# A hybrid attention and GLA block: copies and adds of output-weight blocks queued behind weight loads and probability scalings

## The chip, the cores and the metric

The kernel runs on one core of one Trainium2 chip. The metric is the device time of one execution in microseconds (us). Three executions of the kernel before took 952.4, 955.09 and 950.05 us; their median is 952.4 us. The engines are TensorE (PE, with its weight loads as PEld), VectorE (DVE), ScalarE (ACT), GpSimd (POOL) and SyncE (SP). In this kernel SP issues nearly all transfers, and POOL issues those that add to what lies at the destination.

## What is computed

One layer over 512 tokens of width 2048, all in float32:

```
mod = silu(c) @ w_cond + b_cond            -> shift, scale, gate
h   = rms_norm(x) * (1 + scale) + shift
proj = h @ w_in                            -> aq ak av ag gq gk gv gg lr_f lr_b
A: dilated window attention, 16 heads x 64, three patterns, relative bias; times silu(ag)
B: gated linear attention (GLA), 4 heads, forward and backward; normed, times silu(gg)
y   = concat(A, B) @ w_out                 (512x2048 @ 2048x2048)
out = rms_norm(x + gate * y) * final_gain
```

## The kernel before

**Arithmetic.** Every large product is made of three float32r products: each operand is split into a high part (a rounded copy, made on ACT) and a low part (the rest, made on DVE), and the helper `three` (lines 214 to 217) issues high by high, high by low and low by high.

**Stages.** A first stage works through `w_cond` and the first two weight sets (sa, sb). Then come ten units, each a projection of 512 columns: qk2, qk4, qk6, gk, gv0, gv1, ag0, ag1, gg0, gg1. The function `unit` (line 1000 on) runs a unit in eight groups of two 128-row blocks of weights. At each group it splits the weights of this group and the next (`split_hi` on ACT, `split_lo` on DVE) and asks for the weight loads of the groups two and three ahead (`fetch`, on SP). A unit has 64 ticks, one for each set of three products; at given ticks it issues other work, its side list:

- in qk2, qk4, qk6 and gk the attention of four heads each: scores (L723, L724), softmax (DVE L727, ACT L730, DVE L731), the scaling of the probabilities `p` by the inverse sum on POOL (L735), a transpose on PE (L747) and the products with the values (L761);
- in gv1, ag0, ag1 and gg0 one GLA head each (`gla_head`), with decay products `dc` on POOL (L923);
- from qk6 on, sums for the value bias and the gate (`some_sums`): loads of `rawv` and `rawg` on SP (L831, L797), consumed on DVE (L836, L314);
- in all ten units the block sums described below.

At the start of each unit with attention the heads' keys are laid out: `ks` and `kl` are written in one half of the partitions and carried to the other half by two small transfers on SP (L696, L698). The scores read them.

**The output product and the block sums.** The last stage multiplies by `w_out` with Strassen-like sums: per pair of column blocks seven products, of whose weights four (T1 to T4) are sums and differences of blocks of `w_out`. The blocks are summed in device memory: `sum_start` (L392, on SP) copies 512 KB from a source into a new buffer T, `sum_add` (L397, on POOL) adds a second block to it by a transfer that accumulates. T1 and T3 start from `w_out` itself, T2 from T1, T4 from T2; with two pairs and four row groups there are 32 copies and 32 adds. They stand in one list `sum_ops`, in steps, so that an add or a dependent copy comes some places after what it needs. `SUM_OPS_IN` deals the list out to the units, and `unit` issues the share evenly over its 64 ticks.

**What sets the order.** PE's instructions run in the order of the program. Those of the other engines and queues are put in order by a planner at build time, which may move an instruction ahead of others on its queue when by its own times it is ready and the queue is free; side work is issued with raised priority. The executed order is then fixed: each queue issues in order, and an instruction that waits holds up all behind it.

The list has 64 entries: gv0 and gg1 get 5, ag1 and gg0 get 6, the other six units 7 each.

Of the kernel before, what the change touches and what calls it, by code (L numbers as in the profile page):

```python
# [14 lines left out]
ALU = mybir.AluOpType  # L15
# [105 lines left out]
OUT_SUMS = {"T1": ("11", "12"), "T3": ("12", "22"), "T2": ("T1", "22"), "T4": ("T2", "21")}  # L121
# [57 lines left out]
def block_kernel(ctx: ExitStack, tc: tile.TileContext, a: dict):  # L179
    nc = tc.nc  # L180
# [12 lines left out]
    def T2(name, dt=F32, parts=P):  # L193
        return t2.tile([parts, 512], dt, tag="t2", name=name)

    def B8(name, shape, dt=F32):
        return b8.tile([P] + shape, dt, tag="b8", name=name)
# [4 lines left out]
    def PA(name):  # L202
        return pp.tile([P, 512], F32, tag="pa", bufs=3, name=name)
# [41 lines left out]
    def RAW(name, shape):  # L245
        return wp.tile([P] + shape, F32, tag="raw", bufs=4, name=name)
# [100 lines left out]
    groups = [(u, g) for u in order for g in range(KT // 2)]  # L347
    groups += [("O", s) for s in range(2 * 4 * len(OUT_ORDER))]
    gi = {ug: i for i, ug in enumerate(groups)}
    raws, wts, low = {}, {}, set()  # L350

    def fetch(i):
        if i < len(groups) and i not in raws:
            u, g = groups[i]
            if u == "O":
                raws[i] = out_fetch(g)
            else:
                raws[i] = RAW(f"raw_{u}{g}", [2, 512])
                nc.sync.dma_start(raws[i], a["w_" + u][g])

    def out_block(pair, which, g):

        l, r = OUT_PAIRS[pair]
        j, z = {"11": (l, g), "21": (l, 4 + g), "12": (r, g), "22": (r, 4 + g)}[which]
        return a[f"w_o{j}"][z]

    def out_fetch(s):

        pair, q = divmod(s, 4 * len(OUT_ORDER))
        what, g = OUT_WEIGHTS[OUT_ORDER[q // 4]], q % 4  # L370
        if s % 2 and s >= OUT_DEEP:
            t = op.tile([P, 2, 512], F32, tag="raw", bufs=3, name=f"raw_O{s}")
        else:
            t = RAW(f"raw_O{s}", [2, 512])
        if what in OUT_SUMS:
            d = dsum[pair, what, g]
            nc.sync.dma_start(t.rearrange("p k c -> p (k c)"),
                              bass.AP(d.tensor, d.offset, [[1024, P], [1, 1024]]))
        else:
            nc.sync.dma_start(t, out_block(pair, what, g))  # L380
        return t

    dsum = {}

    def flat(t):
        return bass.AP(t.tensor, t.offset, [[2048, 64], [1, 2048]])

    def sum_start(pair, name, g):
        def go():
            src = OUT_SUMS[name][0]  # L390
            dsum[pair, name, g] = t = dp.tile([64, 2048], F32, tag=f"{name}{pair}{g}", name=f"{name}{pair}{g}")
            nc.sync.dma_start(t, flat(dsum[pair, src, g] if src in OUT_SUMS else out_block(pair, src, g)))  # L392
        return go

    def sum_add(pair, name, g):
        def go():
            nc.gpsimd.dma_start(dsum[pair, name, g], flat(out_block(pair, OUT_SUMS[name][1], g)), accum_op=ALU.add, max_dma_last_dim=8192)  # L397
        return go

    sum_ops = []  # L400
# [23 lines left out]
    def split_hi(i):  # L424
        if i < len(groups) and i not in wts:
            fetch(i)
            u, g = groups[i]
            raw = raws[i].rearrange("p k c -> p (k c)")
            dst = None
            if (u, g) == ("O", len(groups) - gi["O", 0] - 4):  # L430
                t = b8.tile([P, 2, 1024], F32R, tag="b8", name="wlast")
                dst = t[:, 0, :], t[:, 1, :]
            wts[i] = dst or (wp.tile([P, 1024], F32R, tag="whi", name=f"{u}{g}h"),
                             wp.tile([P, 1024], F32R, tag="wlo", name=f"{u}{g}l"))
            act(wts[i][0], raw, AF.Copy)
# [182 lines left out]
    for z in range(2):  # L618
        for e in range(3):
            name = ("mm", "a", 0, 7) if (z, e) == (1, 2) else ("m0", z, e)  # L620
# [3 lines left out]
    for i in range(n):  # L624
        if i > 7:
            mm_task(i)
        st, k, j = chain[i]
# [15 lines left out]
    for i in range(n, 2 * n):  # L643
        mm_task(i)
        st, k, j = chain[i]
# [3 lines left out]
    for w in range(4):  # L649
        for kt in range(4):  # L650
            j, g = w // 2 * 4 + kt, w % 2
# [51 lines left out]
    def attention(pairs):  # L703

        tiles = [(2 * p + j, i) for p in pairs for j in range(2) for i in range(4)]
        gt, pt, pr_ = {}, {}, {}
        heads = [2 * p + j for p in pairs for j in range(2)]

        def g_load(h):
            g = gp.tile([P, 896], F32, tag="g", name=f"g{h}")  # L710
            nc.sync.dma_start(g, bass.AP(grow.tensor, grow.offset + h * 1024, [[1, P], [1, 896]]))
            gt[h] = g

        def score(h, i):
            def go():
                if h % 8 == 0 and i == 0:
                    cat[h // 8] = B8(f"cat{h // 8}", [4, 512])
                if i == 1 and h != heads[-1]:
                    g_load(h + 1)
                qs, ks, kl, _ = stacks[h]  # L720
                q = slice(P * i, P * i + P)
                ps = PA(f"s{h}{i}")
                mm(ps, qs[:, q], ks, start=True, stop=False)  # L723
                mm(ps, qs[:, q], kl, start=False, stop=True)  # L724
                t = T2(f"p{h}{i}")
                st = sm.tile([P, 3], F32, tag="st", name=f"st{h}{i}", bufs=6)
                nc.vector.tensor_tensor_reduce(  # L727
                    out=t, in0=ps, in1=gt[h][:, P * i:P * i + 512], op0=ALU.add, op1=ALU.min,
                    scale=1.0, scalar=3e38, accum_out=st[:, 0:1])
                act(t, t, AF.Exp, bias=st[:, 0:1], scale=-1.0, accum_out=st[:, 1:2])  # L730
                nc.vector.reciprocal(st[:, 2:3], st[:, 1:2])  # L731
                if (h, i) in ((15, 2), (15, 3)):
                    act(t, t, AF.Copy, scale=st[:, 2:3])
                else:
                    nc.gpsimd.tensor_scalar(t, t, st[:, 2:3], 1.0, op0=ALU.mult, op1=ALU.mult)  # L735
                pr_[h, i] = t
            return go

        def turn(h, i):
            def go():  # L740
                half, ii = divmod(i, 2)
                if ii == 0:
                    pt[h, half] = B8(f"pt{h}{half}", [2, 4, 256], F32R)
                t = pr_.pop((h, i))
                pk = PA(f"t{h}{i}")
                for kt in range(4):
                    nc.tensor.transpose(pk[:, kt * P:kt * P + P], t[:, kt * P:kt * P + P], ident)  # L747
                hi = pt[h, half][:, 0, :, P * ii:P * ii + P]
                lo = pt[h, half][:, 1, :, P * ii:P * ii + P]
                src = pk.rearrange("p (k q) -> p k q", k=4)  # L750
                act(hi, src, AF.Copy)  # L751
                tt(lo, src, hi.bitcast(F32), op=ALU.subtract)  # L752
            return go

        def values(h, half):
            def go():
                t = pt.pop((h, half))
                po = PA(f"o{h}{half}")
                for kt in range(4):
                    for w in range(2):  # L760
                        mm(po[:, :256], vv[h // 4][:, kt, h % 4, :], t[:, w, kt, :],  # L761
                           start=kt == 0 and w == 0, stop=kt == 3 and w == 1)
                oh = sm.tile([64, 256], F32, tag="oh", name=f"oh{h}{half}", bufs=1)
                act(oh, po[64:128, :256], AF.Copy)  # L764
                own = stacks[h][3]
                p = h // 2
                dst = cat[p // 4][own, p % 4, 256 - 256 * half:512 - 256 * half]
                tt(dst[:, ::-1], po[0:64, :256], oh, op=ALU.add)  # L768
            return go

        items = []
        n = len(tiles)
        for x in range(n + 4):
            if x < n:
                items.append(score(*tiles[x]))
            if 2 <= x <= n + 1:
                items.append(turn(*tiles[x - 2]))
            if x == n:
                continue
            for v in (x - 4, x - 3) if x == n + 1 else (x - 3,):  # L780
                if 0 <= v < n and tiles[v][1] % 2 == 1:
                    items.append(values(tiles[v][0], tiles[v][1] // 2))
        g_load(heads[0])
        start, span, move0, move1, move_last = ATT_AT
        at = [start + (q + 0.5) / len(items) * span for q in range(len(items))]
        at[0] -= move0
        at[1] -= move1
        at[-1] += move_last
        return list(zip(at, items))
# [366 lines left out]
    for e in "hl":  # L1156
        t = hp.tile([P, KT, 512], F32R, tag="h", name="c_" + e)
# [263 lines left out]
```

## Time and profile before

| | |
|---|---|
| median of three runs | 952.4 us |
| profiled execution | 955.71 us, span 953.9 us |
| granted PE clock, mean | 0.988 |
| PE busy | 922.7 us, 97% of the span |
| DVE, ACT, POOL busy | 656.1, 473.3, 84.5 us |
| SP's transfers (q1) | 191.61 MB, 57.0% of 16 DMA engines |
| POOL's transfers (q0) | 16.84 MB, 9.1% of 16 DMA engines |

The profiled execution lies 3.3 us above the median. Times in a trace count from the start of the span. A row of the timeline gives start, length, engine, line, operation, output and inputs, and in brackets how long the engine had been idle and what ended that. A row of waits gives the total, the number of times and the longest. A row of stages gives the stretch, its length, the busy time of PE, PEld, DVE, ACT and POOL, the granted clock, the share of the DMA engines and GB/s.

### The profile page before, as it was taken

How to read it: one execution, taken by the hardware profiler on the slowest of the kernel's cores; microseconds unless marked ns; L12 is line 12 of the kernel's file. 1: busy time of each engine (PE TensorE's matmuls, PEld its weight loads, DVE VectorE, ACT ScalarE, POOL GpSimd, SP SyncE). 2: the span in 40 equal slices, each digit the busy share in tenths (PEclk: the TensorE clock that was granted, in tenths of full speed). 3: DMA queues.
4: the chain of work that ended last, by engine and by line, in shares of the span. 5: the costliest groups of instructions: out<-in, count | busy, mean ns of one | idle time of the engine just before them, and what ended most of it. 6: DMA issues, size and time to landing. Idle time of an engine off the chain costs nothing.

```text
span 953.9 us, 12126 instructions
## 1 busy us (share of the span) xinstructions
PE 922.7 (97%) x4375; PEld 763.3 (80%) x4375; DVE 656.1 (69%) x960; ACT 473.3 (50%) x770; POOL 84.5 (9%) x120
## 2 busy tenths in 40 slices
PE   8999999989899979999999999999999999999996
PEld 6888888868677858888887888888888888888884
DVE  7988899746555647676643566578597628798486
ACT  5543533635445535565621545454364428555464
POOL 0000000112413312212100000000001000000001
PEclk9999999989999989999999999999999999999998
DMA  9999496979999998353245425355455446966853
GB/s 353 403 411 366 190 366 232 277 211 287 287 291 278 292 265 269 117 174 127 98 156 177 135 76 169 97 176 179 156 173 168 136 138 224 320 210 223 279 173 138
DMA packets 52803, 209.79 MB, mean 220 GB/s; under 512 B 7204, under 2 KB 7492, under 8 KB 45960
## 3 DMA queue, kind: packets, MB, share of 16 engines
q1 hardware_dynamic: 49680, 191.61, 57.0%
q0 software_dynamic: 2624, 16.84, 9.1%
q8 instruction: 34, 0.56, 0.2%
q10 hardware_dynamic: 440, 0.57, 0.2%
q14 instruction: 25, 0.20, 0.1%
HBM read 200.53 MB, written 37.83 MB: 250 GB/s over the span
## 4 chain that ended last, share of the span: by engine, by line
PE 56%; DVE 3%; DMA 1%; issue 1%; ACT 1%; ACTq 0%; DVEq 0%
PE g L217 4%; PE g L216 4%; PE g L215 4%; PE ps_gv L217 3%; PE ps_gv L216 3%; PE ps_gv L215 3%; PE ps_ag L215 3%; PE ps_ag L217 3%; PE ps_ag L216 3%; PE ps_gg L215 2%; PE ps_gg L216 2%; PE ps_gg L217 2%; PE o L761 2%; PE ps_gk L217 2%; PE ps_gk L215 2%; PE ps_gk L216 2%
## 5 line engine op out<-in xcount | busy, mean ns | idle before, releaser
L730 ACT ACTIVATE p<-p,st 128x512 f32<-128x512 f32 x64 | 46.1, 721 | 72.5 <-DVE st L727 70.6
L314 DVE CUSTOM_DVE_ANT_0 cb<-cb,sb,c_bcond 128x2048 f32<-128x2048 f32 (+1 forms) x32 | 73.5, 2296 | 1.5 <-DMA cb<-in_wm 1.2
L727 DVE CUSTOM_DVE_ANT_0 p<-s,g 128x512 f32<-128x512 f32 x64 | 43.9, 688 | 32.6 <-PE s L724 32.4
L735 POOL TENSOR_SCALAR p<-p,st 128x512 f32<-128x512 f32 x62 | 49.3, 808 | 129.3 <-DVE st L731 99.0
L752 DVE TENSOR_TENSOR pt<-t,pt 128x512 fp32r<-128x512 f32 x64 | 43.8, 689 | 21.5 <-ACT pt L751 21.0
L751 ACT ACTIVATE pt<-t 128x512 fp32r<-128x512 f32 x64 | 37.9, 592 | 14.9 <-PE t L747 13.9
L747 PEld LDWEIGHTS t<-c_ident,p 128*128 128x128 f32 x256 | 31.7, 142 | 16.5 <-POOL p L735 8.6
L747 PE MATMUL t<-c_ident,p 128*128 128x128 f32 x256 | 39.6, 278 | 5.6 <-POOL p L735 5.3
L397 POOL DMA_DIRECT2D T<-in_w_o x32 | 25.6, 800 | 202.5 <-DMA T<-in_w_o 131.5
L761 PEld LDWEIGHTS o<-pt,vv 128*128 128x128 f32 x256 | 34.8, 188 | 2.8
L761 PE MATMUL o<-pt,vv 128*128 128x256 f32 x256 | 35.5, 281 | 0.0
L723 PE MATMUL s<-ks,qs 128*128 128x512 f32 x64 | 26.2, 409 | 7.6 <-DMA ks<-ks 7.5
L923 POOL TENSOR_SCALAR dc<-st,sc 128x256 f32<-128x256 f32 x16 | 9.4, 586 | 249.2 <-DVE st L920 244.2
L724 PE MATMUL s<-kl,qs 128*128 128x512 f32 x64 | 26.2, 410 | 4.4 <-DMA kl<-kl 4.3
L314 DVE CUSTOM_DVE_ANT_0 rawg<-rawg,sb,gate 128x1024 f32<-128x1024 f32 x16 | 20.5, 1282 | 13.5 <-DMA rawg<-in_wg 13.4
L731 DVE RECIPROCAL st<-st 128x1 f32<-128x1 f32 x64 | 10.3, 161 | 24.8 <-ACT p L730 24.8
L314 DVE CUSTOM_DVE_ANT_0 rawg<-rawg,sb,c_bcond 128x1024 f32<-128x1024 f32 x16 | 20.5, 1281 | 6.7 <-DMA rawg<-in_wg 6.7
L1246 POOL TENSOR_SCALAR x<-x,rn 128x512 f32<-128x512 f32 x3 | 3.4, 1137 | 216.6 <-ACT rn L1235 216.6
L723 PEld LDWEIGHTS s<-ks,qs 128*128 128x128 f32 x64 | 12.4, 194 | 12.0 <-issue 7.1
L930 ACT ACTIVATE sq<-st,sc 128x256 f32<-128x256 f32 x24 | 12.2, 508 | 18.6 <-DVE st L925 9.3
L768 DVE TENSOR_TENSOR cat<-o,oh 64x256 f32<-64x256 f32 x32 | 13.3, 416 | 8.3 <-ACT oh L764 7.8
L314 DVE CUSTOM_DVE_ANT_0 rawv<-rawv,shb,vbias 128x1024 f32<-128x1024 f32 x8 | 10.2, 1281 | 12.7 <-DMA rawv<-in_wv 12.6
(1519 smaller groups left out, 2976.1 us busy)
## 6 DMA issues: line engine op xcount, KB each, us to landing
cb<-in_wm SPq DMA_DIRECT2D x31, 1024.0 KB, 8.4
T<-in_w_o POOLq DMA_DIRECT2D x32, 512.0 KB, 9.7
rawg<-in_wg SPq DMA_DIRECT2D x32, 512.0 KB, 3.3
raw_O<-T SPq DMA_DIRECT2D x32, 512.0 KB, 4.9
raw_qk<-in_w_qk SPq DMA_DIRECT2D x24, 512.0 KB, 7.9
raw_O<-in_w_o SPq DMA_DIRECT2D x24, 512.0 KB, 4.2
rawb<-in_w_sb SPq DMA_DIRECT2D x16, 512.0 KB, 5.2
T<-in_w_o SPq DMA_DIRECT2D x16, 512.0 KB, 9.8
```

Of the source, the lines that this page charges most:

```text
L215: mm(ps, lh, rh, start=first, stop=False, skip_group_check=more)
L216: mm(ps, ll, rh, start=False, stop=False, skip_group_check=more)
L217: mm(ps, lh, rl, start=False, stop=last, skip_group_check=more)
L314: nc.vector.tensor_tensor_reduce(out=w, in0=w, in1=with_, op0=ALU.mult, op1=ALU.add, scale=1.0, scalar=init, accum_out=dst)
L723: mm(ps, qs[:, q], ks, start=True, stop=False)
L727: nc.vector.tensor_tensor_reduce(out=t, in0=ps, in1=gt[h][:, P * i:P * i + 512], op0=ALU.add, op1=ALU.min, scale=1.0, scalar=3e38, accum_o ...
L730: act(t, t, AF.Exp, bias=st[:, 0:1], scale=-1.0, accum_out=st[:, 1:2])
L735: nc.gpsimd.tensor_scalar(t, t, st[:, 2:3], 1.0, op0=ALU.mult, op1=ALU.mult)
L747: nc.tensor.transpose(pk[:, kt * P:kt * P + P], t[:, kt * P:kt * P + P], ident)
L751: act(hi, src, AF.Copy)
L752: tt(lo, src, hi.bitcast(F32), op=ALU.subtract)
L761: mm(po[:, :256], vv[h // 4][:, kt, h % 4, :], t[:, w, kt, :], start=kt == 0 and w == 0, stop=kt == 3 and w == 1)
```

## The change

Two entries are kept in `last`: the last weight load that `fetch` issued in the program's order, and the last scaling of probabilities. A copy is tied behind the first on SP, an add behind the second on POOL. The tie (`tc.issue_after`) is one of order on the queue alone; nothing waits on a signal that it did not wait on before. The planner may still place the copy or add anywhere later on the queue.

```
-    raws, wts, low = {}, {}, set()
+    raws, wts, low, last = {}, {}, set(), {}
...
-                nc.sync.dma_start(raws[i], a["w_" + u][g])
+                last["load"] = nc.sync.dma_start(raws[i], a["w_" + u][g]).ins
...
     def sum_start(pair, name, g):
...
-            nc.sync.dma_start(t, flat(dsum[pair, src, g] if src in OUT_SUMS else out_block(pair, src, g)))
+            with tc.issue_after(last["load"]):
+                nc.sync.dma_start(t, flat(dsum[pair, src, g] if src in OUT_SUMS else out_block(pair, src, g)))
...
     def sum_add(pair, name, g):
         def go():
-            nc.gpsimd.dma_start(dsum[pair, name, g], flat(out_block(pair, OUT_SUMS[name][1], g)), accum_op=ALU.add, max_dma_last_dim=8192)
+            with tc.issue_after(last["pool"]) if "pool" in last else nullcontext():
+                nc.gpsimd.dma_start(dsum[pair, name, g], flat(out_block(pair, OUT_SUMS[name][1], g)),
+                                    accum_op=ALU.add, max_dma_last_dim=8192)
...
-                    nc.gpsimd.tensor_scalar(t, t, st[:, 2:3], 1.0, op0=ALU.mult, op1=ALU.mult)
+                    last["pool"] = nc.gpsimd.tensor_scalar(t, t, st[:, 2:3], 1.0, op0=ALU.mult, op1=ALU.mult).ins
```

After gk there is no further scaling, so the adds of the later units are tied to the last one of gk. The loads of the output product's own weights don't count as `last["load"]`.

## The prediction

> **What bounds the kernel now.** I read the page's busy shares first, then the busy time stage by stage, then the waits of TensorE (PE) where the stages differ, and last the queues that feed them.
>
> ```profile
> PE 922.7 (97%) x4375; PEld 763.3 (80%) x4375; DVE 656.1 (69%) x960; ACT 473.3 (50%) x770; POOL 84.5 (9%) x120
> ```
>
> PE is busy for 922.7 of 953.9 us, so only its holes and its clock can be won. The next rows cut the span into units: qk2, qk4, qk6 and gk (each a projection with the attention of four heads inside), gv0 with gv1, ag0 with ag1, gg0 with gg1.
>
> ```profile
> 188.50:267.00 78.50, 70.64 (x346) 57.96 (x346) 44.01 (x91) 39.30 (x75) 22.04 (x30) 0.93 0.93 264
> 267.00:337.40 70.40, 67.08 (x354) 55.67 (x353) 42.26 (x89) 37.68 (x72) 20.77 (x28) 1.00 1.02 290
> 337.40:412.60 75.20, 68.82 (x354) 56.79 (x353) 46.84 (x97) 37.71 (x73) 15.01 (x20) 0.95 0.68 206
> 412.60:479.00 66.40, 66.37 (x354) 55.87 (x353) 45.17 (x97) 37.49 (x72) 9.73 (x14) 1.00 0.42 134
> 479.00:585.00 106.00, 106.00 (x502) 86.85 (x501) 52.76 (x68) 39.04 (x60) 1.92 (x4) 1.00 0.43 138
> 585.00:693.00 108.00, 108.00 (x541) 91.62 (x540) 72.84 (x100) 52.64 (x87) 3.84 (x8) 1.00 0.47 155
> 693.00:798.00 105.00, 104.62 (x493) 87.03 (x491) 69.87 (x88) 50.40 (x71) 3.63 (x4) 1.00 0.45 147
> ```
>
> The columns after the length are busy time of PE, PEld, DVE, ACT and POOL, then granted PE clock, DMA share and GB/s. The first four units hold nearly the same PE work (354 matmuls in the records of three of them), yet take 78.5, 70.4, 75.2 and 66.4 us. Against the last, the first three lose 12.1 + 4.0 + 8.8 = 24.9 us. Of that, PE is idle for 7.86 + 3.32 + 6.38 = 17.56 us (length less busy); the other 7.3 us is a lower clock (0.93 and 0.95). Their DMA share is 0.93, 1.02 and 0.68, against 0.42 in gk. What ends the holes, from the waits of PE between 180 and 365 us, and three of the holes:
>
> ```profile
> PE s L723 <- DMA ks<-ks: 7.5, 3, 4.3
> PE t L747 <- POOL p L735: 5.3, 4, 1.9
> PE s L724 <- DMA kl<-kl: 4.3, 1, 4.3
> ...
> 199.18 0.76 PE L723 MATMUL s<-ks,qs 128*128 128x512 f32 x1 [4.34 <-DMA ks<-ks]
> 257.84 0.66 PE L747 MATMUL t<-c_ident,p 128*128 128x128 f32 x4 [1.91 <-POOL p L735]
> 303.88 0.66 PE L747 MATMUL t<-c_ident,p 128*128 128x128 f32 x4 [1.93 <-POOL p L735]
> ```
>
> So 11.8 us wait for small SBUF-to-SBUF transfers (ks, kl) and 5.3 us for POOL's scaling of probabilities. Both trace to the block sums, which are all issued between 168 and 367 us:
>
> ```profile
> L397 POOL DMA_DIRECT2D T<-in_w_o x32: 762/782/1068, 173.5 to 367.1; - x32
> DMA to landing us min/median/max: 7.6/9.7/14.6
> ...
> L392 SPq DMA_DIRECT2D T<-in_w_o x16: 489/539/691, 168.5 to 299.6; - x16
> L392 SPq DMA_DIRECT2D T<-T x16: 467/516/1475, 212.5 to 355.9; - x16
> ...
> 255.82 0.78 POOL L397 DMA_DIRECT2D T<-in_w_o  x1 [9.52 <-DMA T<-T]
> 275.34 0.77 POOL L397 DMA_DIRECT2D T<-in_w_o  x1 [13.59 <-DMA T<-T]
> ```
>
> An add at the head of POOL's queue waits for its copy to land (9.52, 13.59 us) while scalings stand behind it; the hole at 257.84 follows the first of these. And the ks transfer, to landing, in the gk stage (405 to 425 us) and then around qk6 (325 to 360 us):
>
> ```profile
> DMA to landing us min/median/max: 2.2/2.3/2.4
> DMA to landing us min/median/max: 8.1/12.2/14.4
> ```
>
> 2.3 us where no sum is under way, 12.2 us where the DMA engines are full.
>
> **The change part by part.** No work is added or removed: 32 copies (SP) and 32 adds (POOL) stay, in the same list, dealt out as 7, 7, 7, 7, 5, 7, 7, 6, 6, 5 to the ten units. Each copy now stands on SP behind the weight load traced last, each add on POOL behind the scaling traced last. The load traced last is two or three groups ahead of PE, a group being 66.4 / 8 = 8.3 us, so a copy can run at most some 25 us ahead of its place; the adds of the attention units can't pass a scaling. So 28 of the 64 operations stay in the four attention units, 36 go to gv0 and after.
>
> *DMA load.* Against gk's 0.42 the first three units carry (0.93 × 78.5 + 1.02 × 70.4 + 0.68 × 75.2) − 0.42 × 3 × 66.4 = 196 − 84 = 112 us of engine time for about 57 operations (64 less some 7 issued before 188 us), 2 us each. Seven to a unit of 66.4 us then add 14 / 66.4 = 0.21: the attention units fall to about 0.63, gk rises to the same, and the units from gv0 on, 36 × 2 = 72 us more over 319 us, go from 0.45 to 0.68. No stage stays full.
>
> *ks and kl.* At 0.63 I estimate 4 to 6 us to landing: between 2.3 and 12.2, nearer the first, since a queue that is not full empties between operations. The three holes in qk4 and qk6, 11.8 − 4.34 = 7.5 us, begin late after the issue; the first of each:
>
> ```profile
> 264.11 0.48 SPq L696 DMA_DIRECT2D ks<-ks  x1
> 335.08 0.48 SPq L696 DMA_DIRECT2D ks<-ks  x1
> ...
> 275.47 0.47 PE L723 MATMUL s<-ks,qs 128*128 128x512 f32 x1 [1.24 <-DMA ks<-ks]
> 346.75 0.47 PE L723 MATMUL s<-ks,qs 128*128 128x512 f32 x1 [1.95 <-DMA ks<-ks]
> ```
>
> PE came at 274.2 and 344.8, some 10 us after the issue. With 6 us to landing all 7.5 us go. In qk2 the cover is thinner:
>
> ```profile
> 186.03 0.49 SPq L392 DMA_DIRECT2D T<-in_w_o  x1
> 189.29 0.51 SPq L696 DMA_DIRECT2D ks<-ks  x1
> ...
> 185.43 0.81 POOL L397 DMA_DIRECT2D T<-in_w_o  x1 [11.12 <-DMA T<-in_w_o]
> 187.91 0.77 POOL L397 DMA_DIRECT2D T<-in_w_o  x1 [1.67 <-DMA T<-in_w_o]
> 194.84 0.77 POOL L397 DMA_DIRECT2D T<-in_w_o  x1 [6.16 <-DMA T<-in_w_o]
> ```
>
> PE came at 199.18 − 4.34 = 194.84, 5.55 us after the issue at 189.29. A copy three microseconds ahead of ks stays about where it is; the adds of 185.43, 187.91 and 194.84 go to the second half of the unit. Bounds: 0 (all of the wait goes) and 4.34 us plus its share of the clock (it stays). I take 1.0 us as what is left here.
>
> *Scalings.* An add now follows its copy by 4 to 10 places of the list in the attention units (about 9.5 us a place, 66.4 / 7), 38 us or more, against a longest copy of 18.1 us to landing:
>
> ```profile
> DMA to landing us min/median/max: 4.1/11.3/18.1
> ```
>
> So no add waits in front of a scaling, and the 5.3 us go. What an add itself takes on POOL stays: 12 adds of 0.78 us in the attention units, at most 9.4 us if each held PE up and nothing if the 56.7 idle us of POOL in gk (66.4 − 9.73) hide them; I take nothing, since some 28 adds stand among the scalings today and every hole but one of 0.45 us follows an add that waited.
>
> *Clock.* The lower clock follows the holes; with them gone the 7.3 us come back. At one place the row and the notes can be weighed:
>
> ```profile
> 260.00:280.00 20.00, 18.70 (x86) 15.23 (x84) 11.61 (x20) 9.87 (x17) 3.50 (x6) 0.93 1.03 247
> 300.00:320.00 20.00, 18.07 (x99) 15.04 (x98) 10.65 (x26) 10.18 (x21) 6.71 (x9) 1.00 1.00 299
> ```
>
> The hole of 1.91 us at 257.84 is followed by a clock of 0.93, that of 1.93 us at 303.88 by none lost. The Trainium skill, "TensorE: Matmul & The Clock Gate", Part 1, has the clock halved after an idle window of about 3.4 us and full again after a busy one; the trace agrees that holes come first, but a hole of 1.9 us was enough once. By that page three drops at half rate would be worth an estimated 3 × 1.7 = 5.1 us instead of 7.3 and the time 2.2 us higher; I keep the rows.
>
> *Copies on SP.* A copy occupies SP for 0.54 us and may wait there. A T<-T copy must wait for the add before it in the chain of sums, and loads queue behind it. Between add and copy stand at least 5 places but for the last two (4 and 3), more than 28 us; less the 25 us ahead and the 9.7 us of an add, a few could wait some microseconds. The cover is the same two or three groups that the loads run ahead: I take 0. Without that cover the loads would be late for PE, which is the fourth rival.
>
> *The later units.* Here 36 operations are new. PE has no hole from 479 to 693 us and 0.38 us from 693 to 798, but the chain of work passes through DVE and two waits for gate weights:
>
> ```profile
> 681.55 4.62 DMA rawg<-in_wg
> ...
> 687.51 3.15 DMA rawg<-in_wg
> ...
> 715.26 0.55 PE kt L901 x3
> ```
>
> A load takes 3.15 us alone and 4.62 us behind another. A copy in between will stretch some. DVE waits in order, so its weight splits and the gates of the next GLA head come later. Bounds: 0, and for the five units two loads each stretched by 4.62 − 3.15 = 1.5 us and all of it on PE's path, 15 us. PE's full rows before 693 say that most heads have room, this one none: I take 2.5 us. POOL's decay products (dc) could stand behind an add that waits for its copy; they come in a few bursts per unit and POOL is busy for 3.84 of 108 us: nothing.
>
> *Output product.* The last sums (T4 of the second column pair) are wanted in the middle of that pair, after 850 us, and the list ends before 800: no wait.
>
> **The sum.** −24.9 + 1.0 + 2.5 = −21.4 us. The profiled execution has 955.7 us (span 953.9), which gives 934.3; it lies 3.3 us above the median of the runs, 952.4, and on that the forecast is 931.
>
> **The rivals.** *The first stall stays.* For it: ks is still behind a copy on SP's own queue, and the Trainium skill, "DMA: Bandwidth & Descriptors", section Queues, rings and completion order, says that on each DMA engine a row's descriptors are consumed in ring order, so a transfer issued first stays first; no run here shows the order inside a queue. Against: the adds on the other queue are gone. By rows 4.34 us and the clock after it (12.1 us lost in qk2 in all, 7.86 of it idle, so 4.2 for the clock), less the 1.0 already counted: 931 + 7.5 = 938.5.
>
> *The later units give part back.* The upper bound above in place of 2.5: 931 + 12.5 = 943.5. For it: the chain at 681 to 715 us with no room. Against: DMA share 0.45 there and full rows for PE before 693.
>
> *The sums don't move enough.* If loads are issued so early that the copies behind them still crowd together, DMA stays full: 952. Against: loads wait for buffers that PE's progress frees, and the loads of one unit are spread over it already.
>
> *SP is blocked, slower than before.* A T<-T copy waits at the head of SP's queue for an add that now stands behind scalings; loads, ks, kl and bias rows queue behind it. It has happened once:
>
> ```profile
> SPq L392 <- DMA T<-in_w_o: 6.9, 1, 6.9
> ```
>
> Without harm that time. With 16 such copies it decides from 21.4 / 16 = 1.3 us each that reaches PE; at 2 us each it is 931 + 32 = 963, which I take. Against it stand the 28 us between add and copy and the load buffers.
>
> **How the numbers follow.** Chances: forecast 0.50; first stall stays 0.15; later units give back 0.18; no effect 0.07; SP blocked 0.10. About 0.5% (4.8 us) is what a measurement of this kernel can tell from no change. Faster by more: 0.50 + 0.15 + 0.16 = 0.81; within: 0.02 + 0.07 = 0.09; slower: 0.10. The low end is 952.4 − 24.9 less the 2.4 us by which the fastest run shown lies below the median, 925; the high end takes in the third case with as much spread, 946; what is left out is the last two and a little of the third. The likeliest case alone spans 926 to 937.
>
> **What would show it.** Units qk2, qk4 and qk6 at 66 to 68 us each with a clock of 1.00 and a DMA share near 0.63; ks landing within 6 us; no POOL scaling behind an add that waits; copies and adds from about 175 to 790 us; and in the units from gv0 on rows no more than 3 us longer together, with longer waits of DVE for gate weights. The forecast is wrong if PE has holes after 479 us that end with a weight split, or if SP shows long waits at the T<-T copies.

## The result, and the profile after

The changed kernel takes 945.45 us (median of 7 runs, 943.98 to 948.97), the kernel before 952.06 us (median of 7): a ratio of 0.9936, 95% interval 0.9915 to 0.9958. It is faster by 6.6 us where 21 were forecast; the time lies just inside the range, at its slow end. The profiled execution has 948.97 us, its span 947.2 us against 953.9 before.

The stages of the kernel after, cut at the first matmul of each unit: qk2, qk4, qk6, gk, gv0, gv1, ag0 with ag1, gg0. The columns are those of the stage rows above.

```profile
188.30:253.60 65.30, 65.28 (x345) 54.84 (x344) 43.53 (x90) 38.80 (x75) 12.65 (x18) 1.00 0.50 154
253.60:320.00 66.40, 66.38 (x354) 55.84 (x353) 41.90 (x90) 37.46 (x72) 14.13 (x20) 1.00 0.52 156
320.00:390.20 70.20, 68.26 (x354) 56.97 (x353) 46.81 (x97) 37.61 (x73) 14.17 (x19) 0.98 0.71 209
390.20:463.10 72.90, 68.67 (x354) 57.45 (x353) 44.80 (x96) 37.42 (x72) 16.03 (x22) 0.95 0.67 195
463.10:517.50 54.40, 52.78 (x233) 41.13 (x232) 19.10 (x24) 12.26 (x15) 1.55 (x2) 1.00 0.61 188
517.50:577.40 59.90, 56.34 (x272) 46.97 (x271) 33.81 (x44) 27.07 (x46) 5.04 (x8) 0.97 0.66 190
577.40:685.50 108.10, 108.10 (x541) 91.72 (x540) 73.56 (x100) 53.48 (x88) 8.62 (x13) 1.00 0.67 214
685.50:741.40 55.90, 54.35 (x271) 45.82 (x271) 45.28 (x62) 30.43 (x48) 6.04 (x7) 1.00 0.65 198
```

The kernel before has in the units from gv0 on, in its own finer cut (gv0, gv1, gg0):

```profile
479.00:531.30 52.30, 52.30 (x233) 41.30 (x232) 20.17 (x27) 12.28 (x16) 0.00 (x0) 1.00 0.47 153
531.30:585.40 54.10, 54.10 (x271) 45.88 (x270) 32.59 (x44) 26.78 (x46) 1.92 (x4) 1.00 0.40 125
693.60:748.20 54.60, 54.32 (x272) 45.84 (x271) 45.14 (x61) 30.14 (x48) 3.63 (x4) 1.00 0.50 163
```

So qk2, qk4 and qk6 gain 13.2 + 4.0 + 5.0 = 22.2 us, and gk, gv0, gv1 and gg0 lose 6.5 + 2.1 + 5.8 + 1.3 = 15.7 us. The rest is unchanged. The waits of PE have moved as well (after, longest first):

```profile
PE o L764 <- DVE pt L755: 4.2, 1, 4.2
PE z L865 <- DVE ups L1098: 3.5, 1, 3.5
PE sta L525 <- ACT h_hi L471: 2.1, 1, 2.1
PE s L726 <- DVE pt L755: 1.9, 1, 1.9
PE kt L904 <- DVE ki L894: 1.6, 1, 1.6
```

No hole ends with ks, kl or a scaling any more; the new ones end with DVE (the row with ACT lies in the first stage and was there before, with 1.2 us). What DVE was doing shows in the chain of work between 440 and 470 us, and what POOL had just done in its timeline:

```profile
446.06 9.75 DMA rawv<-in_wv
457.27 10.40 DMA rawv<-in_wv
```

```profile
443.17 0.70 POOL L738 TENSOR_SCALAR p<-p,st 128x512 f32<-128x512 f32 x1 [3.45 <-PE t L750]
443.81 5.62 POOL L399 DMA_DIRECT2D T<-in_w_o  x7
483.66 0.77 POOL L399 DMA_DIRECT2D T<-in_w_o  x1 [34.23 <-DMA T<-T]
```

Right behind gk's last scaling on POOL, seven adds go out in 5.6 us. Ten adds went before them and the list has twelve up to gk, so by the count two belong to gk, tied to that scaling, and five to gv0 and gv1, where no later scaling ties them; as far as the executed order shows, the planner let them run ahead as soon as their copies were due. The seven need up to 21.0 us to land. Two loads for the value bias issued meanwhile take 9.75 and 10.40 us in place of 3.1, DVE waits for them in order, and the probabilities' low parts (`pt`), weight splits and gates behind it come late for PE. DVE doesn't catch up: the chain of work stays with its sums and their loads, one after the other, until 531 us, where PE's hole of 3.5 us in gv1 ends.

Theory 1 after this reading: adds that run together fill the DMA engines, loads that an engine waits for in order land late, and PE pays. Theory 2: any sum in these units costs time, by its traffic. Theory 3: the copies' new place on SP is to blame.

### The profile page after: what moved, and what is told of

It reads as the page before. It is cut to its first block, busy times and chain, and to the rows that moved or that the text cites. A ratio compares the mean times of both kernels' runs of the same rounds, so it can differ in the third digit from the quotient of the medians.

```text
span 947.2 us, 12118 instructions
## 1 busy us (share of the span) xinstructions
PE 920.3 (97%) x4375; PEld 762.4 (80%) x4375; DVE 655.3 (69%) x960; ACT 472.8 (50%) x770; POOL 84.3 (9%) x120
## 3 DMA queue, kind: packets, MB, share of 16 engines
HBM read 200.53 MB, written 37.83 MB: 252 GB/s over the span
## 4 chain that ended last, share of the span: by engine, by line
PE 79%; DMA 10%; DVE 5%; issue 3%; ACT 2%; ACTq 0%; DVEq 0%; SPq 0%
DMA rawv<-in_wv 5%; PE ps_qk L215 4%; PE ps_qk L216 4%; PE ps_qk L217 4%; PE g L217 4%; PE g L215 4%; PE g L216 4%; PE stb L217 3%; PE stb L216 3%; PE stb L215 3%; PE ps_ag L217 3%; PE ps_ag L215 3%; PE ps_ag L216 3%; PE t L750 3%; PE o L764 3%
## 5 line engine op out<-in xcount | busy, mean ns | idle before, releaser
L738 POOL TENSOR_SCALAR p<-p,st 128x512 f32<-128x512 f32 x62 | 44.1, 711 | 327.9 <-DVE st L734 280.1
L839 DVE CUSTOM_DVE_ANT_0 rawv<-rawv,shb 128x1024 f32<-128x1024 f32 x8 | 9.8, 1223 | 21.0 <-DMA rawv<-in_wv 18.2
L767 ACT ACTIVATE oh<-o 64x256 f32<-64x256 f32 x32 | 12.2, 382 | 19.8 <-PE o L764 19.0
```

What stands on the lines that cost most here:

```text
L738: last["pool"] = nc.gpsimd.tensor_scalar(t, t, st[:, 2:3], 1.0, op0=ALU.mult, op1=ALU.mult).ins
```

## The experiments

Lengths of the units in us, from the stage rows of each run (cut at the first matmul of each unit), and the time as a ratio to the kernel before on the same chip:

| run | qk2 | qk4 | qk6 | gk | gv0 | gv1 | ag0, ag1 | gg0 | gg1 | median us | ratio (95%) |
|---|---|---|---|---|---|---|---|---|---|---|---|
| before | 78.5 | 70.4 | 75.2 | 66.4 | 52.3 | 54.1 | 108.2 | 54.6 | 43.5 | 952.06 | 1 |
| after | 65.3 | 66.4 | 70.2 | 72.9 | 54.4 | 59.9 | 108.1 | 55.9 | 43.5 | 945.45 | 0.9936 (0.9915 to 0.9958) |
| e1 copies tied | 65.6 | 66.4 | 66.8 | 70.7 | 52.3 | 54.3 | 108.2 | 55.3 | 43.5 | 938.32 | 0.9836 (0.9796 to 0.9876) |
| e2 adds tied | 65.4 | 66.3 | 70.1 | 73.2 | 64.0 | 63.5 | 108.2 | 54.6 | 43.5 | 961.17 | 1.0087 (1.0058 to 1.0116) |
| e3 no sums | 65.3 | 66.3 | 66.6 | 66.3 | 52.3 | 54.1 | 108.2 | 55.0 | 43.5 | 929.83 | 0.9746 (0.9711 to 0.9781) |
| e4 paced | 65.4 | 66.4 | 68.3 | 67.6 | 52.3 | 58.2 | 110.2 | 58.1 | 47.9 | 946.69 | 0.9920 (0.9894 to 0.9947) |
| e5 paced in gv0 | 65.4 | 66.3 | 67.6 | 67.7 | 53.2 | 64.0 | 108.3 | 55.7 | 43.5 | 943.85 | 0.9889 (0.9859 to 0.9918) |
| e6 no DVE sums | 65.4 | 66.3 | 70.4 | 66.4 | 62.9 | 54.1 | 108.2 | 54.7 | 43.5 | 945.28 | 0.9906 (0.9873 to 0.9939) |
| e7 plain adds | 65.3 | 66.3 | 67.0 | 73.3 | 52.3 | 54.1 | 108.1 | 54.3 | 43.5 | 936.55 | 0.9816 (0.9787 to 0.9845) |
| e8 gk free | 67.1 | 66.3 | 67.6 | 67.1 | 52.3 | 60.0 | 108.1 | 55.2 | 43.5 | 937.98 | 0.9831 (0.9803 to 0.9860) |
| e9 dealt early | 73.1 | 66.3 | 67.6 | 66.3 | 52.3 | 54.1 | 110.4 | 59.9 | 43.5 | 945.56 | 0.9894 (0.9856 to 0.9933) |
| e10 mid unit | 65.4 | 66.3 | 66.5 | 70.2 | 52.2 | 54.2 | 108.2 | 59.2 | 43.5 | 937.02 | 0.9823 (0.9787 to 0.9858) |
| e11 gk light | 66.6 | 66.3 | 67.2 | 66.9 | 52.3 | 54.3 | 108.2 | 55.7 | 43.5 | 934.35 | 0.9795 (0.9753 to 0.9837) |
| e12 free from gk | 65.3 | 66.4 | 74.4 | 70.0 | 52.3 | 54.1 | 108.2 | 55.1 | 43.5 | 942.61 | 0.9868 (0.9834 to 0.9902) |

**One half of the change each, e1 and e2.** The edit of e1, against the kernel after:

```
-            with tc.issue_after(last["pool"]) if "pool" in last else nullcontext():
+            with nullcontext():
                 nc.gpsimd.dma_start(dsum[pair, name, g], ...
```

and of e2:

```
-            with tc.issue_after(last["load"]):
+            with nullcontext():
                 nc.sync.dma_start(t, ...
```

> Only the copies are tied behind weight loads; the adds are free again. Theory 1 (the adds of the GLA units, which nothing ties after the last scaling, go out in one burst at the end of gk, fill the DMA engines, and DVE waits in order for value-bias and gate weights): the free adds follow their copies one by one, the burst of seven at the end of gk becomes four or fewer, gk to gv1 lose under half of the 14.4 us that they lose now, but some adds wait for a copy ahead of a scaling in qk2 to qk6: 938 to 945 us in all. Theory 2 (any sum in gk to gv1 costs PE time because of the traffic itself): 942 to 947. Theory 3 (the copies' place on SP, ahead of the loads that DVE waits for, is the cause): gk to gv1 stay as slow as with the full change, 945 or more.

> Only the adds are tied behind scalings; the copies run ahead as before. Theory 1: with all copies early, every add after gk is ready at once, so the burst grows from seven to some ten or more, and gk to gv1 lose more than the 14.4 us of the full change; 950 to 965 us. Theory 2: the traffic in gk to gv1 is about that of the full change less the copies; 943 to 950. Theory 3: no copies are left on SP in gk to gv1, so these units come back to 66, 52 and 54 us; 935 to 940.

The copies' tie alone is worth 0.9836, more than twice the full change; the adds' tie alone makes the kernel slower, 1.0087. That parts the theories. Theory 3 fails, since with the copies on SP gv0 and gv1 are whole in e1, and without them there they are at their worst in e2. Theory 2 fails in the same two units: in e1 they carry as much DMA traffic as after (shares 0.63 and 0.65 against 0.61 and 0.66) and lose at most 0.2 us. Their rows in e1:

```profile
458.40:510.70 52.30, 52.30 (x233) 41.30 (x232) 19.18 (x24) 12.28 (x16) 2.34 (x3) 1.00 0.63 203
510.70:565.00 54.30, 54.30 (x271) 45.80 (x270) 33.68 (x44) 26.76 (x45) 4.29 (x7) 1.00 0.65 184
```

For gk, which keeps 70.7 us in e1, theory 2 stays open until the last experiments. In e2 POOL sends nine adds behind the last scaling:

```profile
443.22 7.20 POOL L399 DMA_DIRECT2D T<-in_w_o  x9
451.52 0.77 POOL L399 DMA_DIRECT2D T<-in_w_o  x1 [1.10 <-DMA T<-in_w_o]
458.43 0.77 POOL L399 DMA_DIRECT2D T<-in_w_o  x1 [6.14 <-DMA T<-T]
477.10 2.37 POOL L399 DMA_DIRECT2D T<-in_w_o  x3 [17.90 <-DMA T<-T]
```

and the waits for value-bias loads in its chain are 9.78, 13.24 and 15.95 us:

```profile
445.48 9.78 DMA rawv<-in_wv
456.72 13.24 DMA rawv<-in_wv
472.49 15.95 DMA rawv<-in_wv
```

In e1 each add follows its own copy, and the copies are spread, so the adds are spread without a tie. The landings of its 32 adds:

```profile
DMA to landing us min/median/max: 4.9/7.1/9.3
```

The longest is 9.3 us, against 21.0 us after. A single add still stretches a load beside it (a value-bias load issued at 474.69 lands in 8.3 us), but DVE isn't late there and PE loses nothing. Some adds wait on POOL ahead of a scaling, as in the kernel before, but no unit from qk2 to qk6 is more than 0.3 us longer than after.

**The floor, e3.** Copies and adds are left out and the output product reads a plain block where it would read a sum.

```
     def sum_start(pair, name, g):
         def go():
+            return
...
     def sum_add(pair, name, g):
         def go():
+            return
...
-            d = dsum[pair, what, g]
-            nc.sync.dma_start(t.rearrange("p k c -> p (k c)"), ...
+            nc.sync.dma_start(t, out_block(pair, OUT_SUMS[what][1], g))
```

> All copies and adds are left out; the output product reads one plain block of the output weights where it would read a sum, so its result differs, with the same loads. All theories: every unit as long as its undisturbed best, qk2 to gk 65 to 67 us each, 952.1 - 24.9 = 927 us. If a unit of gk to gv1 stays long without any sum, the cause is the order of other work, not the sums.

929.83 us, every unit within 0.7 us of the best that any run shows; the ratio 0.9746 is 24.2 us of 952. The 24.9 us read from the stages of the kernel before were thus the sums', and nearly all to be had; the full change takes 6.6 of them.

**Pacing the adds, e4 and e5.** In e4 each add from gv0 on goes behind a small operation on POOL (its mark) that reads DVE's newest sum, whose column is kept in `last["column"]`; e5 ends that with gv0.

```
...
         def go():
+            if last.get("paced"):
+                last["pool"] = nc.gpsimd.tensor_scalar(pace, last["column"], 1.0, 1.0, op0=ALU.mult, op1=ALU.mult).ins
             with tc.issue_after(last["pool"]) if "pool" in last else nullcontext():
...
+    last["paced"] = True
     ps = unit("gv0", ...
...
+    last["paced"] = False      # e5 alone
     ps = unit("gv1", ...
```

> The full change, and from gv0 on each add is also tied behind a one-column operation on POOL that reads the newest gate or value-bias sum of DVE, so that adds can't run ahead of the units they are dealt to. Theory 1: no burst; gk 67 to 69, gv0 52 to 54, gv1 54 to 56 us, in all 931 to 937 us. Theory 2: the same traffic in total, so 942 to 947. Theory 3: the copies are unmoved, 943 to 947.

> As the paced kernel, but only the adds of gv0 are tied behind a one-column operation; from gv1 on adds are tied only behind the last of those. Theory 1 (the burst of adds at the end of gk made the loss, and the paced kernel lost it again because its marks set each add loose at the moment DVE's next gate load goes out): gk and gv0 stay at 67 to 68 and 52 to 53 us as in the paced kernel, ag1 to gg1 come back to 54, 55 to 56 and 43.5; 935 to 940 us. Theory 2 (later units lose whenever adds run in them): ag1 to gg1 stay 8 us too long in all, 944 to 947.

Both missed in the sum, and theory 1 is right where the burst was: gk 67.6 and 67.7 in place of 72.9, gv0 52.3 and 53.2 in place of 54.4. In e5 the units from ag0 on come back as well, as its theory 1 said. In e4 the loss came back in the later units. A mark lets an add go at the moment when DVE has finished a sum, which is when the buffer comes free and the next gate load goes out, so such an add runs beside just the load that DVE waits for next. Three such waits in its chain, where a load takes 3.2 us alone:

```profile
550.89 7.74 DMA rawg<-in_wg
...
641.13 7.38 DMA rawg<-in_wg
...
735.72 8.34 DMA rawg<-in_wg
```

In e5 the burst moved, and the loss with it: five adds go together behind the last mark (POOL's timeline). The value-bias load issued with them at 480.38 us takes 9.43 us and the next one 8.69 us; then a gate load beside a further single add (508.98) takes 10.72 us. All three are in DVE's chain of work, and gv1 has 64.0 us.

```profile
479.38 1.03 POOL L400 TENSOR_SCALAR pace<-vbias 128x1 f32<-128x1 f32 x1 [26.67 <-DVE vbias L314]
480.35 4.04 POOL L402 DMA_DIRECT2D T<-in_w_o  x5
```

```profile
491.20 8.69 DMA rawv<-in_wv
...
508.24 10.72 DMA rawg<-in_wg
```

**Through which engine, e6.** The 15 value-bias and gate sums of DVE in gk, gv0 and gv1 are left out, with their loads kept.

```
+    for z in (vbias, gate, gate0, vbias0):
+        nc.vector.memset(z, 0.0)
...
     def some_sums(name):
+        if name in ("gk", "gv0", "gv1"):
+            r = [sum_work.pop(0)[0] for _ in range(SUMS_IN[name])]
+            return [(max(q - 0.3, 0.1) / len(r), x) for q, x in enumerate(r)]
```

> The full change with all its transfers, but the 15 value-bias and gate sums that DVE makes in gk, gv0 and gv1 are left out while their loads stay; the output differs. Theory 1 (the loss runs through DVE, which waits in order for these loads while they share the DMA engines with the adds): gk to gv1 come back to 66 to 68, 52 to 53 and 54 to 55 us, though seven adds still go out together: 930 to 935 us. Rival (the burst delays the weight loads or the scalings themselves): gk to gv1 stay above 180 us together, 940 or more.

By the numbers the rival came: gk to gv1 take 183.4 us together and the whole 945.28. By the units theory 1 is half right: gk and gv1 are back at 66.4 and 54.1 us, so their losses ran through DVE. (The edit takes away DVE's work on these sums too, some 1.3 us each, but the kernel before does that work in the same units without a hole.) gv0, however, has 62.9 us, with one hole of 8.8 us, and it isn't the rival's weight loads or scalings. There ACT waits in order for a small load of 256 KB that fell into the burst (2.7 us to landing in the kernel before), and keeps back the copies of gk's results:

```profile
ACT lrs L1073 <- DMA lrb<-in_w_lr: 14.2, 1, 14.2
```

So it is not DVE as such. In this case two engines that wait in order for a load beside the run of adds hold up PE: DVE, and without DVE's waits ACT.

**What makes an add heavy, e7.** POOL's transfers copy and don't add.

```
-                                    accum_op=ALU.add, max_dma_last_dim=8192)
+                                    max_dma_last_dim=8192)
```

> The full change, but POOL's transfers copy in place of adding; the output differs. If the read of the destination is what makes an add so heavy beside a load (three passes over device memory where a copy has two): a value-bias load beside one lands in 5 to 6 us in place of 9 to 10, gk to gv1 lose half of the 14.4 us or less, 935 to 940 us. If any transfer of this size does it: the same loss, 943 to 947.

936.55 us, as expected if the accumulation matters: qk6, gv0, gv1 and gg0 are whole. But gk keeps its loss, and the expected sign missed for the first load: the value-bias load issued in the burst (442.69) still takes 9.8 us, only the next one falls to 3.7 us (9.75 and 10.40 after). The landings of the seven in the burst, after (first line) and in e7:

```profile
DMA to landing us min/median/max: 5.2/12.7/21.0
```

```profile
DMA to landing us min/median/max: 3.7/7.7/13.1
```

All seven are issued within 3.1 us, so from the first landing to the last pass about 21.0 − 5.2 + 3.1 = 18.9 us, and 13.1 − 3.7 + 3.0 = 12.4 us in e7: for six steps 3.1 and 2.1 us each. The accumulation makes the burst half as long again, and the longer part of it hits gv0 and gv1. The time of POOL's packets in the DMA engines shows the same over the whole span, after (first line) and in e7:

```profile
q0 software_dynamic: 2624, 16.84, 9.8%
q0 software_dynamic: 2624, 16.84, 5.0%
```

The same packets and bytes take twice the time when they accumulate. Whether the reading of the destination is the reason stays open: both pages count 200.53 MB as read.

**The tie in gk alone, e12.** The adds of gk and later units are not tied.

```
-            with tc.issue_after(last["pool"]) if "pool" in last else nullcontext():
+            with tc.issue_after(last["pool"]) if "pool" in last and "free" not in last else nullcontext():
...
+    last["free"] = True
     ps = unit("gk", ...
```

> The full change up to qk6; the adds dealt to gk and later units are not tied. If it is the tie to the last scalings of gk that gathers the adds into one burst, there is none now, and gk to gv1 take 70 to 71, 52.3 and 54 to 55 us as with the copies alone tied, while qk6 keeps its 70 us: 935 to 940 us. If the burst comes from anything else (the copies' places), gk to gv1 stay at 187 us together and the whole at 943 to 947 us.

gk 70.0, gv0 52.3 and gv1 54.1 us: the burst at gk's end comes from the tie. The whole missed, 942.61 us, because qk6 didn't keep its 70 us. The tie of the earlier units makes a smaller burst at the start of qk6, which costs more here, 74.4 against 70.2 us, as a third add joins it (e12, POOL's timeline):

```profile
314.31 0.69 POOL L738 TENSOR_SCALAR p<-p,st 128x512 f32<-128x512 f32 x1 [4.16 <-DVE st L734]
314.95 1.59 POOL L399 DMA_DIRECT2D T<-in_w_o  x2
320.98 0.77 POOL L399 DMA_DIRECT2D T<-in_w_o  x1 [4.44 <-DMA T<-T]
```

The third add goes as soon as the second T<-T copy has landed; in the order of the list its add is dealt to gk, so it is one of those that e12 leaves free. Free adds run ahead too, but singly, each behind its copy.

**What is left under e1, gk: e8, e9, e10, e11.** All four start from e1. e8 moves the four value-bias sums of gk later; e10 issues each unit's share between 0.25 and 0.85 of the unit; e9 and e11 deal the list out otherwise.

```
-SUMS_IN = {"qk6": 4, "gk": 4, "gv0": 9, "gv1": 2, "ag0": 7, "ag1": 9, "gg0": 9}
+SUMS_IN = {"qk6": 4, "gk": 0, "gv0": 9, "gv1": 4, "ag0": 8, "ag1": 9, "gg0": 9}   # e8
...
-SUM_OPS_IN = {"qk2": 7, "qk4": 7, "qk6": 7, "gk": 7, "gv0": 5, "gv1": 7, "ag0": 7, "ag1": 6, "gg0": 6, "gg1": 5}
+SUM_OPS_IN = {"qk2": 10, "qk4": 10, "qk6": 7, "gk": 2, "gv0": 2, "gv1": 5, "ag0": 8, "ag1": 8, "gg0": 7, "gg1": 5}   # e9
+SUM_OPS_IN = {"qk2": 7, "qk4": 10, "qk6": 9, "gk": 2, "gv0": 5, "gv1": 7, "ag0": 7, "ag1": 6, "gg0": 6, "gg1": 5}   # e11
...
-        return [((q + 0.5) / n, x) for q, x in enumerate(r)]
+        return [(0.25 + 0.6 * (q + 0.5) / n, x) for q, x in enumerate(r)]   # e10
```

> Only the copies tied, and besides the four value-bias sums of gk are moved to the later units (none in gk, 4 in gv1, 8 in ag0, 5 in gg1). Theory 1: with nothing on DVE in gk that waits for a load, gk falls from the 70.7 us that it has with the copies alone tied to 66.3 to 67; the later units give back up to 2 us; 933 to 936 us. If gk stays at 70 us, its loss has another cause (the keys' transfers or the copies on SP).

> Only the copies tied, and each unit's share is issued between a quarter and 0.85 of the unit in place of over all of it, so that few copies fall at the start, where ks and kl are moved and the keys' work stands on DVE. If gk's hole of 3 us comes from sums at the change of units, gk falls to 67 to 68 us and the whole takes 934 to 937 us; if from the value-bias loads beside the adds, it stays near 70 us and 938 us.

> Only the copies tied, and the list dealt out as 10, 10, 7, 2, 2, 5, 8, 8, 7, 5, so that gk and gv0, where DVE and ACT wait in order for loads, have 4 operations in place of 12. If an add does harm only beside a load that an engine waits for in order, gk falls from 70.7 to 67 us or less, qk2 and qk4, whose loads are two groups ahead, stay at 65 to 67 us, and the whole takes 932 to 936 us. If the sums cost time wherever they are dense, qk2 and qk4 grow by what gk loses: 937 to 940 us.

> Only the copies tied, and five operations of gk dealt to qk4 and qk6 (7, 10, 9, 2, 5, 7, 7, 6, 6, 5); the other units keep the share with which they lost nothing under the copies' tie alone. By the theory that an add does harm only beside a load that an engine waits for in order: gk at 66.3 to 67, qk2 to qk6 at 65.7, 66.3 and 67 to 68, the rest unchanged, 933 to 936 us. If qk4 or qk6 grow by what gk gains, 938 us.

e8: gk falls to 67.1 us, but gv1, with two more loads that DVE waits for, rises to 60.0 and the whole misses its range: nothing won, the place of the loss follows the loads. The copies and adds of gk stay in e8, so theory 2 fails in gk as well. e10: gk stays at 70.2, so its hole doesn't come from sums at the change of units (gg0 rises to 59.2 us here, which no experiment explains); in e1 DVE stands at that place for a value-bias load beside an add:

```profile
405.60 1.23 DVE L839 CUSTOM_DVE_ANT_0 rawv<-rawv,shb 128x1024 f32<-128x1024 f32 x1 [3.82 <-DMA rawv<-in_wv]
```

e9: gk, gv0 and gv1 are whole with 9 operations in place of 19, but qk2 has 73.1 us with ten (ks 7.4 to 8.9 us to landing) and gg0 59.9, while qk4, also with ten, stays at 66.3; the whole, 945.56 us, lies above both expected ranges. So density alone isn't what costs time; it did where PE or an engine ahead of it stood waiting for a transfer. e11 leaves those units as they were in e1 and moves five operations from gk to qk4 and qk6: gk 66.9, qk4 66.3, qk6 67.2, 934.35 us, with qk2 0.9 us above what was expected. It has the lowest ratio of the versions that keep all the work, 0.9795 (0.9753 to 0.9837), about 4.5 us from the floor. Its interval overlaps with that of e1, so the gain over e1 isn't clear from the times; in the traces the ten units take 581.0 us against 583.1.

## Why the prediction was right or wrong

**Right: the first three units.** 24.9 − 1.0 = 23.9 us were forecast there, 22.2 came. qk2 and qk4 are at 65.3 and 66.4 us with a clock of 1.00 and a DMA share of 0.50 and 0.52 (0.63 forecast). ks in qk2, between 186 and 200 us, after:

```profile
DMA to landing us min/median/max: 2.2/2.2/2.6
```

and in the kernel before, between 185 and 205 us:

```profile
DMA to landing us min/median/max: 8.9/9.5/9.7
```

So the 1.0 us left for the first stall was too much and the rival *the first stall stays* fell: the copy at 185.76 is still ahead of ks on SP's queue (it lands 5.0 us later, after the first ks has gone out at 189.01), and ks still lands in 2.2 us. The adds were what filled the engines: in e2, where no add runs before 230 us either, ks takes 2.2 us too, and in e1, with adds at 181, 187 and 192 us, 4.3 to 8.0 us. The clock term came back with the holes: the granted clock is 1.00 in qk2 (0.93 before), and in gk and gv1, with their new holes of 4.2 and 3.5 us, it is 0.95 and 0.97.

**Wrong in size: qk6.** 70.2 us in place of 66 to 68. The tied adds of qk4's end and qk6's start meet behind one scaling at 314.3 us, just when ks and kl are sent, and the chain goes through three transfers in a row:

```profile
317.66 8.19 DMA ks<-ks
325.91 5.93 DMA srow<-shiftt
331.90 4.52 DMA shb<-srow
```

The prediction's estimate of 4 to 6 us to landing for ks was an average over a unit; ks is asked for at one moment, and here two adds were in it (6.5 to 8.2 us to landing). In e1, where no tie gathers them, it takes 3.0 to 4.9 us and the unit has 66.8.

**The step that failed: the cost where sums are new, 2.5 us.** The sum had one term for it, 2.5 us for the later units. gv0, gv1 and gg0 lost 9.2 us, and gk, for which the sum had no term at all, lost 6.5: 15.7 us together. Three premises were wrong. First, the sum took 36 operations to stay in gv0 and after because the list deals them there; but the adds after gk are tied to nothing that comes later, and a tie holds an instruction back, not in its place. Part of them ran forward to the end of gk and met the adds that the tie had kept back. e12 shows that gathering, and e4 that gk (67.6) and gv0 (52.3) lose little or nothing without the burst. Second, the prediction let gk's DMA share rise to 0.63 (0.67 came) and priced only ks, kl and the scalings there, although DVE waits for value-bias loads in gk already in the kernel before. Without the burst at its end, in e1 and e12, gk still loses 4.3 and 3.6 us, with a hole of 3.0 and 2.5 us behind such a wait of DVE. Third, the upper bound of 15 us took 1.5 us for each of ten loads, the price of a load behind another load. A load beside a run of adds takes 9 to 10 us, and in e2 up to 16, so 6 to 13 us more than the 3.1 us alone. PE's full rows in these units were read as room; they only showed that nothing had pressed there yet. One sign that the prediction named for being wrong did come: PE waits after 479 us for the weight splits of gv0 (`gv05l` and `gv06l`, 0.3 and 1.4 us).

**The rivals.** *The later units give part back* is what happened in kind, and its 943.5 us lies near the 945.45 by luck: its 15 us stood for the units from gv0 on, which lost 9.2, and gk's 6.5, which it didn't have, made up the rest; and the loss came by a burst where the rival had spread collisions. *SP is blocked* did not come: the copies are not among SP's waits, and no hole ends with them. *The sums don't move enough* fell with the DMA shares above.

**The scalings.** No add waits in front of a scaling that PE needs, as forecast; but e1, without the adds' tie, has qk2 to qk6 just as good. The tie of the adds, half of the change, was thus costed as free and useful, and costs about a hundredth of the time (0.9936 against 0.9836, some 9.5 us).

## What to carry to other kernels

Tying the start of a chain of background transfers to work that is itself spread spreads the rest as well; tying each later link too gathers the links at the last thing they are tied to. Ask of each such tie what it does when the work that it is tied to runs out. When traffic is moved into a stage, look there for every engine that waits in order for a load, and price the wait by the load beside a burst of what is moved, not by the mean share of the DMA engines.

## What was not expected of the hardware

A load issued just behind an add lands late. In the kernel after, three transfers of 512 KB go out within 1.1 us: a weight load at 483.34, an add at 483.66 and a value-bias load at 484.48. The weight load, ahead of the add, lands in 3.3 us; the add takes 9.1 us and the value-bias load 9.0 us:

```profile
DMA to landing us min/median/max: 9.0/9.0/9.0
```

A load alone takes 3.1 us, and the add at 265.85 us, with little beside it (the load before it lands 0.8 us after the add's issue, the next one goes out 3.5 us after it), takes 4.9 us:

```profile
DMA to landing us min/median/max: 4.9/4.9/4.9
```

One after the other the three would take 3.1 + 4.9 + 3.1 = 11.1 us by these figures; together they are done 10.1 us after the first was issued.

By contrast a copy of the same size on SP, 3 us ahead of ks, did ks no harm (2.2 us to landing). And an order that sets an add loose by the event that also frees a load buffer (e4) makes the collision regular: DVE waits 65.3 us for gate loads there, against 32.0 us in the kernel after.
